# Weighting and splitting the state space inputs in small steps, and taking the mixers' elementwise work off GpSimd

## The chip, the core and the metric

The kernel runs on one core of a Trainium2 chip. A core has five engines with a queue each: TensorE (PE in the profile, with its weight loads as PEld), VectorE (DVE), ScalarE (ACT), GpSimd (POOL) and SyncE (SP, which issues DMAs). Each engine works through its own instructions in order and waits on semaphores for the others. The metric is the device time of one execution in microseconds, over several runs of the same program.

## What is computed

The reference is a model of two layers on 512 tokens of width 1024, in float32. Each layer is a mixer and a gated feed-forward network with a short convolution, both with a residual and an RMS norm ahead of them. The mixer of layer 0 joins a dilated window attention (12 heads in three groups) and a latent attention (12 heads). The mixer of layer 1 joins a state space model (16 heads in two groups, in four chunks of 128 tokens) and a stick-breaking attention (8 heads). The parts that the change touches, cut to what matters:

```python
# rotary embedding, softmax (layer 0)
x1 * cos - x2 * sin, x2 * cos + x1 * sin
p = exp(scores - m); out = (p / sum(p)) @ v
...
# state space model (layer 1), per chunk of 128 tokens
xbc = silu(causal_dwconv(xbc, conv_w, conv_b))      # 12 tiles of 128 channels
xdt = x * dt[..., None]
cs = cumsum(dt * a)
y_diag = einsum(cb[..., None] * exp(cs_l - cs_s), xdt)          # masked, causal
states = einsum(b, exp(cs_end - cs), xdt)
h = h * exp(cs_end) + states                        # over the chunks
y = y_diag + einsum(c, h_before, exp(cs)) + x * d_skip
...
# stick breaking (layer 1)
out = exp(log_w) @ v
```

## The kernel before

Activations lie with 128 channels on the partitions and the 512 tokens along the free dimension. Products run as three TensorE products of a high and a low part: every operand is split into a rounded float32r copy (ACT) and the rest (DVE or POOL), by `split` (L259), `wchunk` (L214) and `token_split` (L620). A weight chunk of 128 outputs is loaded by one DMA on SP into one of two buffers, split, and used in eight pieces of three 512 column matmuls (`proj_pieces`, L637); a piece is one step of a `Stream` (L119).

TensorE's order is written out by hand: `InOrder` (L93) chains its instructions as the program issues them. The other engines' instructions are placed by a planner, which takes dependences, buffers and its own estimate of durations into account, so a statement's place in the source sets its order there only in part. Where ACT must keep an order (its table of functions has to be loaded anew between Silu and Exp), `after` (L240) adds an edge.

A `Stream` holds the projections that still have to run. `fill(n)` (L169) takes n steps, and so places projection work between the latency bound steps of the heads. `defer(n, f)` (L155) puts f on a list, to be called n steps later; `_tick` (L159) counts all entries down, but calls only from the front of the list, so an entry that is due waits for an older one that is not.

**Layer 0's mixer** (L644). `run_qk` (L719) makes rotated queries and keys: ACT copies the projection out (L729), DVE multiplies it by the cosine in permuted order (L730), four DMAs on SP swap the halves (L733), and POOL multiplies the swapped copy by the sine (L734) and adds it (L735). There are 12 of them. The cosine and sine tiles are scaled by the norm's factor on POOL (L704). A softmax block (L572) goes: DVE masks and takes the maximum (L578), ACT takes exp with the sum (L581), DVE the reciprocal (L582), POOL scales by it (L583). There are 64 blocks, 128 to 512 wide; their probabilities are transposed on TensorE (L116), split into `pth` and `ptl` (L600, L601, L951, L952) and used.

**Layer 1's state space model** (`ssd`, L1118). The stream runs 12 convolutions (`run_conv`, L1137): tiles 0 to 7 are the inputs x, 8 and 9 the matrices B, 10 and 11 C. Each does its projection, then four steps on DVE and ACT (L1144 to L1150), Silu (L1152), and 12 steps later its transposes (`conv_tail`, L1122). `run_dt` makes the step sizes; 2 steps later `softplus` (L1184) starts, a chain of some 20 small operations on DVE; 12 steps later `summed` (L1213) takes their cumulative sums on TensorE, and 3 steps later `rows` (L1226) brings them into rows. After the last convolution (L1276) three exponentials follow (L1279), and then `prepare(0)` (L1285) for all four chunks of the first group: x times dt (`xd`, L1292, on POOL and DVE in turn), the split into `xdt` (L1296, L1297), x times d_skip (L1300, POOL), and x times dt times the decay to the chunk's end (L1302, POOL) with its split into `xe` (L1303).

Then come 16 heads (L1422). Ahead of a head stand `states` (L1307, the chunk's state, carried on with a product on POOL, L1318) and `past` (L1323, the output of earlier chunks, added on POOL, L1334), as the table `prior` (L1408) says; `weights` (L1338) makes the decay weights `sg`, `mh` of the head two places on, `apply` (L1354) multiplies them by `xdt` and adds the result to `xs`. At head 4 `prepare(1)` runs, for the second group at once. From head 8 on the gates follow (`silus`, `gate`, `gate_sums`, `gate_norm`).

**Stick breaking** (L1441). Per head and bank of blocks: `score`, with ACT and DVE on `ab` and a selection on POOL (`strict`, L1508), `sums` with another selection, the split of the weights into `wh` (L1559, DVE) and `wl` (L1560, POOL), and `apply`.

In the two feed-forward networks `self.lo` is POOL: there the low parts of the weights (L221) and one product (L528) are POOL's. In the mixers `self.lo` is DVE.

## Time and profile before

| | us |
|---|---|
| median of 3 runs | 1465.1 (1463.52 to 1468.44) |
| profiled execution | 1463.86 |
| its span, first to last instruction | 1462.1 |
| mean granted TensorE clock | 0.985 |
| stages: layer 0's mixer | 0 to 338 |
| layer 0's feed-forward network | 338 to 700 |
| convolutions of the state space model | 700 to 790 |
| its heads | 790 to 905 |
| stick breaking, with the end of the mixer | 905 to 1095 |
| layer 1's feed-forward network | 1095 to 1462 |

Times in the views are microseconds from the span's start, durations of one instruction nanoseconds; busy time is the time in which an engine has an instruction under way. A row of the stages' view has the stretch, its length, then for each engine busy time and, in brackets, its number of instructions, then the granted clock, the DMA engines' share and GB/s. A row of groups has the line, engine, operation, what is written from what, the shape, the count, the busy time, the mean duration, and the idle time of the engine before these instructions with what ended it. A row of waits names who waited for whom, the total, the number of times and the longest.

### The profile page before, as it was taken

How to read it: one execution, taken by the hardware profiler on the slowest of the kernel's cores; microseconds unless marked ns; L12 is line 12 of the kernel's file. 1: busy time of each engine (PE TensorE's matmuls, PEld its weight loads, DVE VectorE, ACT ScalarE, POOL GpSimd, SP SyncE). 2: the span in 40 equal slices, each digit the busy share in tenths (PEclk: the TensorE clock that was granted, in tenths of full speed). 3: DMA queues.
4: the chain of work that ended last, by engine and by line, in shares of the span. 5: the costliest groups of instructions: out<-in, count | busy, mean ns of one | idle time of the engine just before them, and what ended most of it. 6: DMA issues, size and time to landing. Idle time of an engine off the chain costs nothing.

```text
span 1462.1 us, 18180 instructions
## 1 busy us (share of the span) xinstructions
PE 1388.7 (95%) x6796; PEld 1146.8 (78%) x6796; DVE 863.6 (59%) x1362; ACT 663.2 (45%) x1085; POOL 597.1 (41%) x391
## 2 busy tenths in 40 slices
PE   7899899899999999999988898998999999999997
PEld 5777687687888888888877677787888888888886
DVE  7878678746555555122668987678555555552124
ACT  5557457535433333222446465777344333333222
POOL 2454445303655555444102420434215555554441
PEclk9999999999999999999999999999999999999998
DMA  4421212122322322333222111111233233223333
GB/s 166 120 62 55 69 55 69 39 81 73 101 93 95 101 101 85 105 92 95 92 72 73 44 44 58 46 58 40 62 101 101 87 102 101 91 97 94 100 98 98
DMA packets 40264, 121.22 MB, mean 83 GB/s; under 512 B 5232, under 2 KB 8304, under 8 KB 40176
## 3 DMA queue, kind: packets, MB, share of 16 engines
q1 hardware_dynamic: 38160, 117.92, 25.4%
q10 hardware_dynamic: 2016, 2.14, 0.5%
q8 instruction: 54, 0.88, 0.3%
q14 instruction: 34, 0.28, 0.1%
HBM read 114.80 MB, written 2.10 MB: 80 GB/s over the span
## 4 chain that ended last, share of the span: by engine, by line
PE 80%; DVE 12%; ACT 4%; issue 3%; POOL 1%; DMA 1%; DVEq 0%; SPq 0%; ACTq 0%; POOLq 0%
PE proj L113 50%; PE o L113 19%; PE z L113 5%; PE s L113 3%; PE t L116 2%; DVE wlo L221 2%; PE t L113 1%; ACT whi L219 1%; DVE mh L265 1%; DVE sg L1351 0%; DVE cv L1150 0%; DVE xs L1366 0%; DVE xl L331 0%; DVE s L578 0%; DVE rot L730 0%
## 5 line engine op out<-in xcount | busy, mean ns | idle before, releaser
L221 POOL TENSOR_TENSOR wlo<-wraw,whi 128x1024 fp32r<-128x1024 f32 (+1 forms) x135 | 315.2, 2336 | 323.7 <-ACT whi L219 323.7
L219 ACT ACTIVATE whi<-wraw 128x1024 fp32r<-128x1024 f32 (+3 forms) x219 | 222.2, 1015 | 365.0 <-PE proj L113 328.7
L113 PE MATMUL proj<-xh,whi 128*128 128x512 f32 x844 | 343.0, 406 | 8.8 <-ACT xh L330 6.7
L113 PE MATMUL proj<-xh,wlo 128*128 128x512 f32 x844 | 334.1, 396 | 1.4 <-DVE wlo L387 1.1
L113 PE MATMUL proj<-xl,whi 128*128 128x512 f32 x844 | 333.9, 396 | 1.2 <-DVE xl L331 1.2
L113 PE MATMUL proj<-act,whi 128*128 128x512 f32 (+1 forms) x748 | 219.3, 377 | 0.0
L113 PEld LDWEIGHTS proj<-xh,whi 128*128 128x128 f32 x844 | 161.3, 191 | 41.0 <-ACT xh L330 8.7
L113 PEld LDWEIGHTS proj<-xh,wlo 128*128 128x128 f32 x844 | 160.9, 191 | 37.6 <-DVE wlo L387 1.5
L113 PEld LDWEIGHTS proj<-xl,whi 128*128 128x128 f32 x844 | 161.2, 191 | 31.3 <-DVE xl L331 3.1
L113 PEld LDWEIGHTS proj<-act,whi 128*128 128x128 f32 x748 | 137.7, 188 | 25.8
L113 PE MATMUL o<-xh,wlo 128*128 128x512 f32 x368 | 143.4, 390 | 0.0
L113 PE MATMUL o<-xh,whi 128*128 128x512 f32 x368 | 143.3, 389 | 0.0
L113 PE MATMUL o<-xl,whi 128*128 128x512 f32 x368 | 143.2, 389 | 0.0
L113 PE MATMUL proj<-act,wlo 128*128 128x512 f32 (+1 forms) x374 | 140.8, 376 | 0.0
L583 POOL TENSOR_SCALAR s<-s,st 128x512 f32<-128x512 f32 (+1 forms) x64 | 81.2, 1274 | 109.4 <-DVE st L582 82.3
L366 DVE TENSOR_TENSOR x<-x,proj 128x512 f32<-128x512 f32 x31 | 21.2, 684 | 171.0 <-PE proj L113 170.9
L221 DVE TENSOR_TENSOR wlo<-wraw,whi 128x1024 fp32r<-128x1024 f32 (+3 forms) x84 | 100.0, 1190 | 27.3 <-ACT whi L219 26.3
L524 DVE SCALAR_TENSOR_TENSOR cv<-gt,cols,cv 128x511 f32<-128x511 f32 x44 | 94.3, 2148 | 35.9 <-ACT cv L523 35.9
L528 POOL TENSOR_TENSOR sl<-sl,rsr 128x512 f32<-128x512 f32 x44 | 57.8, 1313 | 94.3 <-ACT sl L527 94.3
L527 ACT ACTIVATE sl<-cv 128x512 f32<-128x512 f32 x44 | 27.8, 631 | 127.3 <-DVE cv L525 127.3
L533 DVE TENSOR_TENSOR up<-sl,o 128x512 f32<-128x512 f32 x44 | 30.3, 688 | 91.8 <-POOL sl L528 91.8
L265 DVE TENSOR_TENSOR act<-up,act 128x512 fp32r<-128x512 f32 x44 | 63.3, 1438 | 29.3 <-ACT act L264 29.3
(305 smaller groups left out, 2250.9 us busy)
## 6 DMA issues: line engine op xcount, KB each, us to landing
wraw<-in_g SPq DMA_DIRECT2D x44, 512.0 KB, 3.3
wraw<-in_u SPq DMA_DIRECT2D x44, 512.0 KB, 3.3
wraw<-in_d SPq DMA_DIRECT2D x32, 448.0 KB, 3.3
wraw<-in_wqk SPq DMA_DIRECT2D x20, 512.0 KB, 3.5
wraw<-in_d SPq DMA_DIRECT2D x17, 512.0 KB, 3.5
wraw<-in_wx SPq DMA_DIRECT2D x12, 512.0 KB, 3.4
wraw<-in_wv SPq DMA_DIRECT2D x10, 512.0 KB, 3.6
wraw<-in_wz SPq DMA_DIRECT2D x8, 512.0 KB, 3.3
```

What stands on the lines that cost most here:

```text
L113: return self._put(self.b.nc.tensor.matmul(*args, **kw))
L116: return self._put(self.b.nc.tensor.transpose(*args))
L219: nc.scalar.activation(hi[:, :n], raw[:, :n], AF.Copy)
L221: (eng or self.lo).tensor_tensor(lo[:, :n], raw[:, :n], hi[:, :n].bitcast(F32), op=ALU.subtract)
L265: nc.vector.tensor_tensor(lo, src, hi.bitcast(F32), op=ALU.subtract)
L366: self.nc.vector.tensor_tensor(self.x[m], self.x[m], ps, op=ALU.add)
L524: nc.vector.scalar_tensor_tensor(c[:, 1:], gt[:, : T - 1], col_(1), c[:, 1:], op0=ALU.mult, op1=ALU.add)
L527: nc.scalar.activation(s, c, AF.Silu)
L528: nc.gpsimd.tensor_tensor(s, s, r, op=ALU.mult)
L533: nc.vector.tensor_tensor(u, s, pu, op=ALU.mult)
L583: nc.gpsimd.tensor_scalar(t, t, rl, None, op0=ALU.mult)
```

## The change

It has five parts.

1. In the mixers, POOL's elementwise work goes to other engines: the scaling of the softmax to ACT (L583); the scaling of cosine and sine (L704), the product with the sine and the sum of the rotation (L734, L735), the product with the carried state (L1318), the sum of `past` (L1334) and the low part of stick breaking's weights (L1560) to DVE. POOL keeps the selections of stick breaking, some squares and mask copies at the start, and its work in the feed-forward networks.
2. `prepare` is cut into `decayed(g, c)` (x times the product of step size and decay, and its split) and `prepare(g, c, q)` (half of a chunk's heads: x times dt, its split, x times d_skip), all on DVE and ACT. `decayed` takes x times one factor, since `tok[:, 3]` is multiplied by `tok[:, 0]` beforehand.
3. For the first group both run as stream items without matmuls, after convolutions 5 and 6; for the second group they stand ahead of heads 2 to 9, by the table `early`. `past` of the second group moves to heads 10 to 12.
4. The three exponentials run as a stream item between convolutions 3 and 4, and the Silus of later convolutions are ordered behind them.
5. `_tick` calls every entry that is due, and `summed` is due after 24 steps in place of 12. The buffers of `xdt` become two sets of 4 in place of one of 8.

```diff
     def _tick(self):
         for d in self.late:
             d[0] -= 1
-        while self.late and self.late[0][0] <= 0:
-            self.late.pop(0)[1]()
+        for d in [d for d in self.late if d[0] <= 0]:
+            self.late.remove(d)
+            d[1]()
...
-        nc.gpsimd.tensor_scalar(t, t, rl, None, op0=ALU.mult)
+        nc.scalar.activation(t, t, AF.Copy, scale=rl)
...
         for t in (cr, sr):
-            nc.gpsimd.tensor_tensor(t, t, r, op=ALU.mult)
+            nc.vector.tensor_tensor(t, t, r, op=ALU.mult)
...
-                nc.gpsimd.tensor_tensor(sw, sw, sr, op=ALU.mult)
-                nc.gpsimd.tensor_tensor(view(t), view(t), view(sw, False), op=ALU.add)
+                nc.vector.tensor_tensor(sw, sw, sr, op=ALU.mult)
+                nc.vector.tensor_tensor(view(t), view(t), view(sw, False), op=ALU.add)
...
                 self.silu = nc.scalar.activation(c, c, AF.Silu)
+                for x in exps:
+                    self.after(self.silu, x)
...
-        XD = dict(tag="xdt", bufs=8)
+        XD = [dict(tag=f"xdt{q}", bufs=4) for q in range(2)]
...
+        def run_exps():
+            def run(w):
+
+                for t, src, scale in ((tok[:, 2], tok[:, 1], -1.0), (tok[:, 3], tok[:, 3], 1.0), (cdec, tot, 1.0)):
+                    exps.append(nc.scalar.activation(t, src, AF.Exp, scale=scale))
+                    self.after(exps[-1], self.silu)
+                nc.vector.tensor_tensor(tok[:, 3], tok[:, 3], tok[:, 0], op=ALU.mult)
...
+        def run_prepare(g, *cs):
+            def run(w):
+                for c in cs:
+                    if c < NB - 1:
+                        decayed(g, c)
+                    for q in range(2):
+                        prepare(g, c, q)
...
-            self.stream.defer(12, summed)
+            self.stream.defer(24, summed)
...
+        def decayed(g, c):
+
+            xd = sub.tile([P, T], F32, tag="xd", name=self.nm("xd"), bufs=2)
+            nc.vector.tensor_tensor(xd.rearrange("p (h d) -> p h d", h=8),
+                                    xs[g][:, c].rearrange("p (h d) -> p h d", h=8),
+                                    tok[:, 3, c, g * 8 : g * 8 + 8, None].to_broadcast([P, 8, 64]), op=ALU.mult)
+            xde[g, c] = self.split(xd, sub, "xe", bufs=6)
+
+        def prepare(g, c, q):
+
+            h0 = g * 8 + 4 * q
+            x4 = xs[g][:, c, q * 256 : q * 256 + 256].rearrange("p (h d) -> p h d", h=4)
+            xd = sub.tile([P, 4, 64], F32, tag=("xq", "xd")[q], name=self.nm("xq"), bufs=1 + q)
+            nc.vector.tensor_tensor(xd, x4, tok[:, 0, c, h0 : h0 + 4, None].to_broadcast([P, 4, 64]), op=ALU.mult)
+            sp = sub.tile([P, 4, 2, 64], F32R, name=self.nm("xdt"), **XD[q])
+            nc.scalar.activation(sp[:, :, 0, :], xd, AF.Copy)
+            nc.vector.tensor_tensor(sp[:, :, 1, :], xd, sp[:, :, 0, :].bitcast(F32), op=ALU.subtract)
+            xdt[g, c, q] = sp
+            nc.vector.tensor_tensor(x4, x4, dbc[:, h0 : h0 + 4, None].to_broadcast([P, 4, 64]), op=ALU.mult)
...
-                                  + [run_conv(f) for f in range(2, 8)] + others)
+                                  + [run_conv(2), run_conv(3), run_exps(), run_conv(4), run_conv(5), run_prepare(0, 0, 1),
+                                     run_conv(6), run_prepare(0, 2, 3), run_conv(7)] + others)
...
-                (nc.vector if c % 2 else nc.gpsimd).tensor_tensor(xd, x8, tq(0), op=ALU.mult)
...
-                nc.gpsimd.tensor_tensor(cur.rearrange("p (h d) -> p h d", h=8),
+                nc.vector.tensor_tensor(cur.rearrange("p (h d) -> p h d", h=8),
...
-            nc.gpsimd.tensor_tensor(xs[g][:, c], xs[g][:, c], tt, op=ALU.add)
+            nc.vector.tensor_tensor(xs[g][:, c], xs[g][:, c], tt, op=ALU.add)
...
+        for hh, f, *x in ((2, decayed, 1, 0), (3, decayed, 1, 1), (4, decayed, 1, 2),
+                          (4, prepare, 1, 0, 0), (5, prepare, 1, 1, 0), (6, prepare, 1, 2, 0), (7, prepare, 1, 3, 0),
+                          (8, prepare, 1, 0, 1), (8, prepare, 1, 1, 1), (9, prepare, 1, 2, 1), (9, prepare, 1, 3, 1)):
+            early.setdefault(hh, []).append((f, *x))
...
-                            (5, past, 0, 3), (6, states, 1, 0), (7, states, 1, 1), (8, past, 1, 1),
-                            (9, states, 1, 2), (10, past, 1, 2), (11, past, 1, 3)):
+                            (5, past, 0, 3), (6, states, 1, 0), (7, states, 1, 1), (10, past, 1, 1),
+                            (9, states, 1, 2), (11, past, 1, 2), (12, past, 1, 3)):
...
-        prepare(0)
...
-            if hh == 4:
-                prepare(1)
+            for f, *x in early.get(hh, ()):
+                f(*x)
...
-                nc.gpsimd.tensor_tensor(wl[:, :w], ab[:, :w], wh[:, :w].bitcast(F32), op=ALU.subtract)
+                nc.vector.tensor_tensor(wl[:, :w], ab[:, :w], wh[:, :w].bitcast(F32), op=ALU.subtract)
```

More of the change, by code (lines that the diff above doesn't have):

```diff
@@ L1181, in ssd @@
         nc.vector.tensor_tensor(sel, self.ident[:, 0:16], self.ident[:, 32:48], op=ALU.add)
-        ready = []
+        ready, exps = [], []
+        def run_exps():
[4 more added lines that the diff above has]
+                nc.vector.tensor_tensor(tok[:, 3], tok[:, 3], tok[:, 0], op=ALU.mult)
+                return
+                yield
+            return "exps", lambda: None, run
+        def run_prepare(g, *cs):
[5 more added lines that the diff above has]
+                        prepare(g, c, q)
+                return
+                yield
+            return f"p{g}{cs[0]}", lambda: None, run
         def softplus():
@@ L1263, in run_cb @@
             return f"cb{g}", lambda: None, run
+        xdt, xde = {}, {}
+        def decayed(g, c):
[14 more added lines that the diff above has]
+            nc.vector.tensor_tensor(x4, x4, dbc[:, h0 : h0 + 4, None].to_broadcast([P, 4, 64]), op=ALU.mult)
         st = self.stream = Stream([run_conv(8), run_conv(10), run_conv(9, "o"), run_dt(), run_conv(11, "o"),
                                    run_conv(0)] + [run_cb(0), run_conv(1), run_cb(1)]
-                                  + [run_conv(f) for f in range(2, 8)] + others)
+                                  + [run_conv(2), run_conv(3), run_exps(), run_conv(4), run_conv(5), run_prepare(0, 0, 1),
+                                     run_conv(6), run_prepare(0, 2, 3), run_conv(7)] + others)
         cm = sub.tile([P, P], BF16, tag="cm", name="cm")
@@ L1277, in ssd @@
         assert ready
-        for t, src, scale in ((tok[:, 2], tok[:, 1], -1.0), (tok[:, 3], tok[:, 3], 1.0), (cdec, tot, 1.0)):
-            self.after(nc.scalar.activation(t, src, AF.Exp, scale=scale), self.silu)
         st.fill(4)
-        xdt, xde = {}, {}
-        def prepare(g):
-            xds = []
-            for c in range(NB):
-                x8 = xs[g][:, c].rearrange("p (h d) -> p h d", h=8)
-                tq = lambda k: tok[:, k, c, g * 8 : g * 8 + 8, None].to_broadcast([P, 8, 64])
-                xd = sub.tile([P, 8, 64], F32, tag="xd", name=self.nm("xd"), bufs=2)
-                (nc.vector if c % 2 else nc.gpsimd).tensor_tensor(xd, x8, tq(0), op=ALU.mult)
-                for q in range(2):
-                    h4 = slice(4 * q, 4 * q + 4)
-                    sp = sub.tile([P, 4, 2, 64], F32R, name=self.nm("xdt"), **XD)
-                    nc.scalar.activation(sp[:, :, 0, :], xd[:, h4], AF.Copy)
-                    nc.vector.tensor_tensor(sp[:, :, 1, :], xd[:, h4], sp[:, :, 0, :].bitcast(F32), op=ALU.subtract)
-                    xdt[g, c, q] = sp
-                nc.gpsimd.tensor_tensor(x8, x8, dbc[:, g * 8 : g * 8 + 8, None].to_broadcast([P, 8, 64]), op=ALU.mult)
-                if c < NB - 1:
-                    nc.gpsimd.tensor_tensor(xd, xd, tq(3), op=ALU.mult)
-                    xde[g, c] = self.split(xd.rearrange("p h d -> p (h d)"), sub, "xe", bufs=6)
         state = {}
@@ L1405, in gate_norm @@
                                                op0=ALU.mult, op1=ALU.mult)
-        prior, later = {}, {}
+        prior, later, early = {}, {}, {}
+        for hh, f, *x in ((2, decayed, 1, 0), (3, decayed, 1, 1), (4, decayed, 1, 2),
+                          (4, prepare, 1, 0, 0), (5, prepare, 1, 1, 0), (6, prepare, 1, 2, 0), (7, prepare, 1, 3, 0),
+                          (8, prepare, 1, 0, 1), (8, prepare, 1, 1, 1), (9, prepare, 1, 2, 1), (9, prepare, 1, 3, 1)):
+            early.setdefault(hh, []).append((f, *x))
         for hh, f, g, c in ((0, states, 0, 0), (1, states, 0, 1), (2, past, 0, 1), (3, states, 0, 2), (4, past, 0, 2),
-                            (5, past, 0, 3), (6, states, 1, 0), (7, states, 1, 1), (8, past, 1, 1),
-                            (9, states, 1, 2), (10, past, 1, 2), (11, past, 1, 3)):
+                            (5, past, 0, 3), (6, states, 1, 0), (7, states, 1, 1), (10, past, 1, 1),
+                            (9, states, 1, 2), (11, past, 1, 2), (12, past, 1, 3)):
             prior.setdefault(hh, []).append((f, g, c))
-        prior[8].append((silus, 0))
+        prior.setdefault(8, []).append((silus, 0))
         prior[14] = [(silus, 1)]
```

6 lines of the change are left out of this document (3 added, 3 removed).

## The prediction

> **What bounds the kernel now.** I read the busy shares and the chain that ended last, then PE's waits, then the stages the change touches.
>
> ```profile
> PE 1388.7 (95%) x6796; PEld 1146.8 (78%) x6796; DVE 863.6 (59%) x1362; ACT 663.2 (45%) x1085; POOL 597.1 (41%) x391
> ...
> PE 80%; DVE 12%; ACT 4%; issue 3%; POOL 1%; DMA 1%; DVEq 0%; SPq 0%; ACTq 0%; POOLq 0%
> ```
>
> PE's order is written out by hand, PE is busy 1388.7 of 1462.1 us, and the chain is PE's wherever PE is not waiting for DVE (12%). So an edit gains only what it takes out of PE's idle time. The stages (columns: length, then busy us of PE, PEld, DVE, ACT, POOL, then the granted clock):
>
> ```profile
> 60.00:338.00 278.00, 253.49 (x1523) 207.96 (x1522) 202.99 (x480) 157.60 (x323) 115.16 (x86) 0.99 0.21 63
> ...
> 700.00:750.00 50.00, 46.14 (x224) 37.82 (x223) 35.61 (x71) 25.33 (x42) 3.40 (x3) 0.93 0.23 77
> 750.00:790.00 40.00, 40.00 (x194) 33.26 (x194) 29.71 (x38) 20.81 (x31) 3.94 (x3) 1.00 0.26 83
> 790.00:830.00 40.00, 32.31 (x151) 25.29 (x150) 35.28 (x47) 23.05 (x55) 18.32 (x15) 0.91 0.14 50
> 830.00:870.00 40.00, 36.41 (x180) 28.58 (x179) 36.02 (x57) 24.05 (x52) 13.39 (x10) 0.96 0.12 40
> 870.00:905.00 35.00, 31.72 (x185) 26.64 (x185) 29.49 (x61) 20.84 (x41) 1.66 (x1) 1.00 0.18 60
> 905.00:1045.00 140.00, 130.18 (x647) 108.37 (x647) 102.26 (x170) 93.46 (x162) 54.56 (x73) 0.98 0.15 48
> ```
>
> 60 to 338 is the even mixer, 700 to 790 the convolutions, 790 to 905 the state space heads, 905 to 1045 stick breaking. From 700 to 905 PE idles 3.86 + 0 + 7.69 + 3.59 + 3.28 = 18.4 us. The clock falls too: (1 - 0.93) x 50 = 3.5, 0.09 x 40 = 3.6, 0.04 x 40 = 1.6, together 8.7 us. So 27 us are lost here, 7.4 in the first stage and 19.8 from 790 on; PE's own work is 205 - 27 = 178 us. What ends the long waits (total, times, longest):
>
> ```profile
> PE s L113 <- DVE sp L1211: 3.9, 1, 3.9
> ...
> PE o L113 <- DVE xdt L1297: 6.4, 2, 3.9
> ...
> PE o L113 <- DVE ptl L601: 5.1, 4, 1.8
> ...
> PE t L116 <- POOL s L583: 2.1, 3, 1.1
> ```
>
> The first is the softplus chain, not done when `summed` comes up; the second is `prepare(0)`, in one burst ahead of the first `apply`. In that burst:
>
> ```profile
> 797.32 0.68 DVE L1351 TENSOR_TENSOR sg<-sg,cb 128x512 f32<-128x512 f32 x1
> 797.92 1.53 DVE L265 TENSOR_TENSOR mh<-sg,mh 128x512 fp32r<-128x512 f32 x1
> ...
> 800.82 0.68 DVE L1315 COPY stt<-t 128x512 f32<-128x512 f32 x1
> 801.42 0.67 DVE L265 TENSOR_TENSOR mh<-sg,mh 128x512 fp32r<-128x512 f32 x1
> 802.02 1.52 DVE L1292 TENSOR_TENSOR xd<-xs,tok 128x512 f32<-128x512 f32 x1
> ```
>
> Back to back, a 512 wide DVE operation takes 0.60 us from start to start (801.42 to 802.02). The same `mh` takes 1.53 us in one place and 0.67 in another: DVE stands still while POOL holds something both need.
>
> **The softplus chain.** `summed` goes from 12 to 24 pieces, and the new `_tick` lets `softplus` (due after 2 pieces) run without waiting for older entries of the list. One piece is three matmuls, by the chain of waits:
>
> ```profile
> 384.38 5.44 PE proj L113 x24
> ```
>
> 5.44 / 24 = 0.227 us each, 0.68 a piece. DVE is 3.9 us late; 12 more pieces are some 8 us, and `softplus` itself starts earlier, since its entry no longer stands behind the transposes of a convolution that are due after 12 pieces. What is late next would be the three exponentials and `rows`; they stand two convolutions later. Gain 7 of the 7.4 us (bounds 4 to 7.4).
>
> **The state space inputs.** Groups from 700 to 905 (xcount | busy, mean ns | idle):
>
> ```profile
> L265 DVE TENSOR_TENSOR mh<-sg,mh 128x512 fp32r<-128x512 f32 x16 | 13.3, 834 | 0.9 <-ACT mh L264 0.9
> L1366 DVE TENSOR_TENSOR xs<-o,xs 128x256 f32<-128x256 f32 x32 | 13.3, 417 | 2.1 <-POOL xs L1334 1.2 <-PE o L113 0.5
> L1297 DVE TENSOR_TENSOR xdt<-xd,xdt 128x256 fp32r<-128x256 f32 x16 | 10.7, 711 | 0.5 <-ACT xdt L1296 0.5
> L265 DVE TENSOR_TENSOR ph<-stt,ph 128x512 fp32r<-128x512 f32 x6 | 6.5, 1081 | 0.7 <-ACT ph L264 0.7
> L265 DVE TENSOR_TENSOR xe<-xd,xe 128x512 fp32r<-128x512 f32 x6 | 5.6, 952 | 0.0
> L1292 DVE TENSOR_TENSOR xd<-xs,tok 128x512 f32<-128x512 f32 x4 | 5.3, 1319 | 0.0
> ...
> L1334 POOL TENSOR_TENSOR xs<-xs,yof 128x512 f32<-128x512 f32 x6 | 10.0, 1669 | 23.4 <-DVE yof L1332 23.4
> L1300 POOL TENSOR_TENSOR xs<-xs,hb 128x512 f32<-128x512 f32 x8 | 9.6, 1202 | 2.9 <-DVE xd L1292 2.6
> L1302 POOL TENSOR_TENSOR xd<-xd,tok 128x512 f32<-128x512 f32 x6 | 6.8, 1144 | 24.4 <-ACT tok L1280 16.7 <-DVE xdt L1297 7.7
> L1318 POOL TENSOR_TENSOR stt<-stt,cdec 128x512 f32<-128x512 f32 x4 | 5.6, 1404 | 8.5 <-DVE stt L1320 5.7 <-DVE stt L1315 2.8
> ```
>
> DVE gains 6 + 6 + 4 = 16 operations of 0.60 us (L1334, L1302, L1318): 9.6. A 256 wide one is 417 ns less the same 0.08 of overlap, 0.34 us: L1300 becomes 16 of them (5.4), and L1292 becomes 16 in place of DVE's 4 of 512 (5.4 - 2.4 = 3.0). Together +18.0 us. Against that stand the waits for POOL, mean over clean: `mh` 16 x 0.15, `xdt` 16 x 0.29, `ph` 6 x 0.40, `xe` 6 x 0.27, `xd` 4 x 0.64 = 13.6 us. (The clean values are 0.68 for 512 and 0.42 for 256, from the rows above.) DVE so goes from 166.1 to 170 us beside 178 us of PE work: the load hardly grows, but it has no room. The ACT copies stay 16 and no DMA is added. The places fit the buffers: `prepare(1, c, 0)` at heads 4 to 7 takes the buffers that heads 0 to 3 have read, `prepare(1, c, 1)` at heads 8 and 9 those of heads 4 to 7, and each is needed one to four heads later, a head being some 7 us (115 / 16); so no wait comes in there unless DVE itself runs a head behind. In DVE's queue these 0.34 us pieces stand ahead of `sg` and `mh` of the next weights, for which PE waits, but never more than some 2 us of them at a time, where the burst held 2 `xd`, 8 `xdt` and 3 `xe`, 2 x 1.32 + 8 x 0.71 + 3 x 0.95 = 11. About 11.6 us of it (`prepare(0)` and its three `decayed`) now fall between convolution 5 and the heads, where DVE has a quarter free; PE may pay 1 us. The nearest row for what remains is 870 to 905, POOL nearly silent and DVE 84% busy: PE idles 3.28 of 35, 9%. Over some 105 us of heads that leaves 10 of the 19.8 us. Gain 10 - 1 = 9 (bounds 0, with DVE as the bound, to 19.8). The exponentials placed between convolutions cost two more table loads:
>
> ```profile
> L581 ACT ACT_TABLE_LOAD  x1: 1283/1283/1283, 69.4 to 69.4; - x1
> ```
>
> 2.6 us on ACT, 20.81 of 40 busy there; behind them waits one Silu, whose transposes come 12 pieces later: nothing. Without that cover, 2.6.
>
> **The even mixer.** Durations (min/median/max, and from issue to landing):
>
> ```profile
> L733 SPq DMA_DIRECT2D sw<-raw x48: 507/584/1465, 43.3 to 228.9; - x48
> L734 POOL TENSOR_TENSOR sw<-sw,sin x12: 1282/1292/1692, 47.3 to 233.8; 128x512 f32<-128x512 f32 x12
> L735 POOL TENSOR_TENSOR rot<-rot,sw x12: 1372/1559/1919, 48.7 to 236.7; 128x512 f32<-128x512 f32 x12
> ...
> POOL sw L734: 20.8, 5
> ...
> DMA to landing us min/median/max: 1.9/2.0/3.9
> L583 POOL TENSOR_SCALAR s<-s,st 128x512 f32<-128x512 f32 (+1 forms) x64 | 81.2, 1274 | 109.4 <-DVE st L582 82.3
> L264 ACT ACTIVATE qk<-rt 128x512 fp32r<-128x512 f32 x12 | 7.6, 630 | 3.9 <-DVE rt L773 3.9
> L730 DVE TENSOR_TENSOR rot<-proj,cos 128x512 f32<-128x512 f32 x12 | 11.9, 994 | 0.1
> L872 DVE TENSOR_TENSOR kl<-knp,kh 64x512 fp32r<-64x512 f32 x12 | 10.6, 880 | 0.8 <-ACT kh L871 0.6
> ```
>
> The 64 scalings go to ACT, at most 64 x 0.63 = 40 us on 157.60 of 278, and each softmax is ready 0.6 us sooner. In ACT's queue each now waits for DVE's reciprocal, with Exp, `pth` and `whi` behind it. DVE takes 14 plain products (two of L704) at 0.60 and 12 permuted sums, as L730 does, at 0.9: 19 us, less waits for POOL of perhaps 0.2 x 12 (`kl`) and as much again elsewhere: net +14 on 202.99 of 278. And it takes over a wait: four copies in a row on SP, 3 x 0.58, then 2.0 to land, come to 4 us, for which POOL sat idle 20.8 us before 5 of the 12; the other 7 it covered with scalings. In DVE's queue `ptl`, `vt` and `wlo` stand behind it. If the order puts it far enough back, it is free; right behind L730 it costs some 3 us x 12 = 36. I take 0.75 each, 9 us of DVE, and a third of it on PE: +3. Bounds: -9 (the `ptl` and `s` waits gone, 5.1 + 2.1, and some clock) to +24 (two thirds of 36).
>
> **Stick breaking.** 24 subtractions (L1560) go from POOL to DVE at most at 0.60: +14 us on 102.26 of 140, less some waits; POOL's selections, which stay, no longer stand behind them. The 384 wide ones, two thirds of the 24:
>
> ```profile
> L1560 POOL TENSOR_TENSOR wl<-ab,wh 128x384 fp32r<-128x384 f32 x16 | 18.6, 1162 | 11.3 <-DVE wh L1559 9.9 <-PE proj L113 1.4
> ```
>
> Each product of weights and values is so ready some 0.6 us sooner, and DVE carries 14 us more; PE idles 9.8 of 140 us here, and I let the two nearly cancel: -1 (bounds -5, half of that idle time, to +8, the added DVE work as far as no wait for POOL goes away and half of it shows).
>
> **Sum.** -7 - 9 + 3 - 1 = -14 us on the profiled execution's 1463.9, which is 1.2 below the median of 1465.1: 1451 on the median's scale.
>
> **Rivals.**
> (a) All of it works: DVE's queue is freer than its sum says and the softmaxes gain: -7 - 15 - 7 - 2 = -31, 1434. For it: 13.6 us of waits for POOL vanish just where PE waits. Against: DVE at 170 of 178.
> (b) DVE becomes the bound of the heads: only the first 7 us and 1 us of stick breaking come, the mixer takes 3: 1460. For it: DVE is 88 and 90% busy from 790 to 870.
> The Trainium skill, Perfetto Trace Analysis, Optimizing Scalar/DVE Operations, speaks for (b): where DVE is saturated, work should go off it, even to GpSimd, though the two share a port, so that moving between them may not help. By that rule the time would be that of (b). The trace bears it out in half: DVE is nearly full, but 1.53 against 0.67 us shows that a move off POOL gives waits back.
> (c) Slower: the rotations' products stand in DVE's queue ahead of their copies. Price 2 us of PE each, 24 us, in place of 3: 1472. It decides from 17 us on, 1.4 us a rotation. For it: the 20.8 us of POOL; against: DVE has other work to be placed ahead.
> (d) No change: stalls are only handed to the next stage, 1465.
>
> **Chances.** Forecast 0.42, (a) 0.22, (b) 0.12, (c) 0.13, (d) 0.11. A difference under 0.3%, 4.4 us, can't be told from none here. Faster 0.42 + 0.22 + 0.12 less 0.02 for (b)'s upper edge = 0.74, within 0.13, slower 0.13. The range reaches to (a) and halfway to (c): 1433 to 1467.
>
> **What would show it.** Right: no wait of PE for `sp`, full clock from 700 to 905, that stage near 189 us, DVE about 90% busy in it, `mh` and `ph` near 0.68 us. Wrong: DVE idle ahead of L734 with a DMA as its releaser; DVE at 97% among the heads; ACT idle ahead of L583; PE waiting for `xdt` again.

## The result, and the profile after

| | before | after |
|---|---|---|
| median, us (4 runs each) | 1465.28 (1463.52 to 1468.44) | 1454.86 (1453.63 to 1456.0) |
| profiled execution, us | 1463.86 | 1454.47 |
| its span, us | 1462.1 | 1452.7 |
| mean granted clock | 0.985 | 0.991 |

The ratio is 0.9919, with a 95% interval of 0.9899 to 0.9939: 10.4 us faster, where 14 were forecast. The page of the changed kernel, in the same two lines as before (busy time by engine; the chain that ended last):

```profile
PE 1384.7 (95%) x6796; PEld 1142.2 (79%) x6796; DVE 880.2 (61%) x1457; ACT 697.2 (48%) x1151; POOL 413.2 (28%) x249
...
PE 79%; DVE 12%; ACT 5%; issue 2%; DMA 1%; POOL 0%; SPq 0%; DVEq 0%; ACTq 0%; POOLq 0%
```

POOL lost 184 us of work (597.1 to 413.2); DVE gained 17, ACT 34. The chain hardly looks different, so the stages have to tell. Here both kernels are cut where PE's own program passes from one part to the next, so that a row holds the same matmuls in each (the counts agree but for a few lost records). The six rows are layer 0's mixer, its feed-forward network, the convolutions, the heads, stick breaking, the rest; the columns are those of the stages' view above. Before:

```profile
0.00:337.10 337.10, 302.39 (x1748) 246.89 (x1749) 249.94 (x563) 188.41 (x369) 134.43 (x107) 0.99 0.26 79
337.10:717.50 380.40, 379.50 (x1690) 314.26 (x1689) 172.64 (x178) 130.78 (x166) 188.13 (x93) 1.00 0.30 95
717.50:789.20 71.70, 67.84 (x324) 55.57 (x323) 51.76 (x82) 38.11 (x59) 3.94 (x3) 0.95 0.23 76
789.20:908.30 119.10, 103.76 (x527) 82.93 (x524) 103.12 (x170) 69.55 (x148) 33.38 (x25) 0.96 0.15 49
908.30:1042.40 134.10, 125.07 (x625) 104.48 (x626) 99.47 (x161) 91.23 (x160) 54.56 (x73) 0.97 0.15 47
1042.40:1462.10 419.70, 410.12 (x1891) 342.69 (x1889) 186.68 (x212) 145.12 (x185) 182.69 (x91) 0.99 0.31 97
```

After:

```profile
0.00:343.60 343.60, 304.79 (x1749) 246.83 (x1750) 261.55 (x589) 220.06 (x433) 16.37 (x17) 0.99 0.26 78
343.60:722.40 378.80, 377.86 (x1690) 312.97 (x1689) 172.80 (x178) 130.91 (x166) 188.12 (x93) 1.00 0.30 95
722.40:793.30 70.90, 67.00 (x324) 54.38 (x323) 57.64 (x108) 43.80 (x71) 0.00 (x0) 0.98 0.23 77
793.30:905.10 111.80, 103.03 (x526) 84.05 (x523) 96.25 (x189) 66.23 (x138) 0.00 (x0) 0.95 0.16 52
905.10:1033.50 128.40, 122.41 (x624) 101.65 (x625) 104.63 (x184) 91.19 (x160) 26.05 (x49) 1.00 0.16 49
1033.50:1452.70 419.20, 409.65 (x1891) 342.31 (x1889) 187.37 (x213) 145.00 (x185) 182.69 (x91) 0.99 0.30 97
```

A row gives two things. Its length less PE's busy time is PE's **idle time**. And because the matmuls are the same, a difference in PE's busy time is read here as time lost to a **lower clock**. After less before:

| stage | length | idle | busy (clock) |
|---|---|---|---|
| layer 0's mixer | +6.5 | 34.7 to 38.8: +4.1 | +2.4 |
| feed-forward network | -1.6 | 0 | -1.6 |
| convolutions | -0.8 | 3.9 to 3.9: 0 | -0.8 |
| heads | -7.3 | 15.3 to 8.8: -6.6 | -0.7 |
| stick breaking | -5.7 | 9.0 to 6.0: -3.0 | -2.7 |
| rest | -0.5 | 0 | -0.5 |
| sum | -9.4 | -5.5 | -3.9 |

So the two stages of the state space model give 8.1 us, not 16; stick breaking gives 5.7, not 1; and the mixer takes 6.5, not 3. The 1.6 us of layer 0's feed-forward network, where the change touches nothing, are read as chance of the clock: that stage takes 380.4 us in two of the fourteen profiles of this document (before and b_stick) and 378.7 to 378.8 in the others.

What ends PE's waits after (total, times, longest). Convolutions:

```profile
PE t L116 <- ACT cv L1153: 3.9, 2, 2.4
```

Heads:

```profile
PE o L113 <- DVE mh L266: 6.1, 4, 3.0
```

Layer 0's mixer, before (the wait for `s` on POOL is in the prediction) and after:

```profile
PE proj L113 <- DVE vt L759: 4.5, 4, 1.4
PE t L116 <- DVE ptl L952: 2.9, 1, 2.9
PE s L113 <- DVE qk L265: 2.4, 1, 2.4
PE t L116 <- DVE v L629: 1.4, 3, 0.7
```

```profile
PE proj L113 <- DVE vt L760: 5.6, 5, 1.6
PE s L113 <- DVE qk L266: 3.8, 2, 2.8
PE t L116 <- DVE ptl L953: 3.8, 1, 3.8
PE t L116 <- ACT s L584: 3.7, 5, 1.4
PE t L116 <- DVE v L630: 2.9, 4, 0.9
```

The waits for `sp` and for `xdt` are gone, as forecast. In the convolutions a Silu (L1153) has taken the place of `sp`, for the very same 3.9 us; in the heads `mh` is what is late. In the mixer PE waits a little longer for each of five things, 6.5 us more in all; two other waits became shorter (`ptl` of L601, now L602, 5.1 to 2.6, and `rot`, 3.6 to 1.8).

The new wait in the convolutions can be read instruction by instruction. ACT's timeline of the changed kernel (start, length, what it does, in brackets the idle time ahead of it and its releaser):

```profile
766.78 1.28 ACT L1191 ACT_TABLE_LOAD   x1
...
775.77 1.28 ACT L1153 ACT_TABLE_LOAD   x1 [1.42 <-DVE cv L1151]
777.06 0.63 ACT L1153 ACTIVATE cv<-cv 128x512 f32<-128x512 f32 x1
```

And PE's, just behind it:

```profile
777.74 1.11 PE L116 MATMUL t<-ident,cv 128*128 128x128 f32 x4 [2.39 <-ACT cv L1153]
...
779.51 0.63 PE L113 MATMUL proj<-xh,wlo 128*128 128x512 f32 x1
779.94 0.63 PE L113 MATMUL proj<-xh,whi 128*128 128x512 f32 x1
...
781.32 0.39 PE L113 MATMUL proj<-xl,whi 128*128 128x512 f32 x1
781.55 0.39 PE L113 MATMUL proj<-xh,wlo 128*128 128x512 f32 x1
```

The table, which ACT had changed for the exponentials (L1191), is loaded back for Silu only when DVE has finished the convolution's last tap, and DVE carries 5.9 us more in this stage (51.76 to 57.64). So the load's 1.28 us stand on the path, and PE waits 2.39. Behind that wait the matmuls come 0.43 us apart (779.51 to 779.94), where they come 0.23 apart later (781.32 to 781.55): the stall costs a stretch at half clock as well.

### The profile page after: what moved, and what is told of

It reads as the page before. It is cut to its first block, busy times and chain, and to the rows that moved or that the text cites. A ratio compares the mean times of both kernels' runs of the same rounds, so it can differ in the third digit from the quotient of the medians.

```text
span 1452.7 us, 17971 instructions
## 1 busy us (share of the span) xinstructions
PE 1384.7 (95%) x6796; PEld 1142.2 (79%) x6796; DVE 880.2 (61%) x1457; ACT 697.2 (48%) x1151; POOL 413.2 (28%) x249
## 4 chain that ended last, share of the span: by engine, by line
PE 79%; DVE 12%; ACT 5%; issue 2%; DMA 1%; POOL 0%; SPq 0%; DVEq 0%; ACTq 0%; POOLq 0%
PE proj L113 49%; PE o L113 19%; PE z L113 5%; PE s L113 2%; DVE wlo L222 2%; PE t L116 2%; PE t L113 1%; ACT whi L220 1%; DVE cv L1151 1%; ACT s L584 1%; DVE xl L332 0%; ACT s L582 0%; DVE x L367 0%; DMA sw<-raw 0%; DVE ab L1559 0%
## 5 line engine op out<-in xcount | busy, mean ns | idle before, releaser
L113 PEld LDWEIGHTS proj<-xh,wlo 128*128 128x128 f32 x844 | 160.2, 190 | 37.5 <-DVE wlo L388 1.5
L222 DVE TENSOR_TENSOR wlo<-wraw,whi 128x1024 fp32r<-128x1024 f32 (+3 forms) x84 | 95.6, 1138 | 28.7 <-ACT whi L220 27.9
L113 PEld LDWEIGHTS proj<-act,wlo 128*128 128x128 f32 x374 | 70.4, 188 | 12.9
```

Source lines behind the costliest of these rows:

```text
L113: return self._put(self.b.nc.tensor.matmul(*args, **kw))
L222: (eng or self.lo).tensor_tensor(lo[:, :n], raw[:, :n], hi[:, :n].bitcast(F32), op=ALU.subtract)
```

## The experiments

Two theories of the state space burst are put against each other. **Work on POOL**: the state space burst was slow because POOL held DVE up, and taking work off POOL made the heads faster (that spreading the burst does it was put to a_burst). **Place of the exponentials**: the burst was slow because it could not begin until the exponentials behind the last Silu had run, and what the change gained there it gained by moving those. Twelve kernels were run; each ratio is to the kernel before, measured beside it. The kernel before had medians of 1465.2, 1465.6, 1466.4 and 1468.0 us in the four sets, so medians of different sets are best compared by their ratios.

| kernel | median, us | ratio (95%) |
|---|---|---|
| b_softplus | 1458.17 | 0.9946 (0.9927 to 0.9965) |
| b_stick | 1459.46 | 0.9961 (0.9947 to 0.9975) |
| b_even | 1473.05 | 1.0049 (1.0034 to 1.0065) |
| b_two | 1452.12 | 0.9892 (0.9876 to 0.9909) |
| b_exps | 1463.95 | 0.9992 (0.9978 to 1.0006) |
| a_burst | 1455.78 | 0.9930 (0.9903 to 0.9958) |
| a_ssd_pool | 1452.82 | 0.9916 (0.9891 to 0.9940) |
| a_edge | 1455.38 | 0.9932 (0.9912 to 0.9951) |
| a_tail16 | 1455.29 | 0.9931 (0.9908 to 0.9955) |
| a_even_pool | 1448.47 | 0.9884 (0.9866 to 0.9902) |
| a_rot_pool | 1449.79 | 0.9886 (0.9862 to 0.9911) |
| best | 1449.52 | 0.9887 (0.9865 to 0.9908) |

Names with b_ are the kernel before with one part of the change, names with a_ the changed kernel with one part undone or altered. PE's idle time by stage, worked out from each one's stage rows as above:

| kernel | mixer | convolutions | heads | stick breaking |
|---|---|---|---|---|
| before | 34.7 | 3.9 | 15.3 | 9.0 |
| after | 38.8 | 3.9 | 8.8 | 6.0 |
| b_softplus | 34.7 | 0.0 | 15.3 | 9.8 |
| b_stick | 34.5 | 3.9 | 15.3 | 5.9 |
| b_even | 36.8 | 3.9 | 15.7 | 9.8 |
| b_two | 33.1 | 0.0 | 15.3 | 6.0 |
| b_exps | 33.8 | 7.5 | 9.7 | 9.8 |
| a_burst | 37.3 | 3.9 | 8.8 | 5.9 |
| a_ssd_pool | 37.7 | 2.2 | 9.0 | 5.9 |
| a_edge | 37.0 | 3.0 | 10.7 | 6.0 |
| a_tail16 | 37.5 | 0.0 | 13.8 | 6.0 |
| a_even_pool | 32.7 | 3.9 | 10.1 | 6.0 |
| a_rot_pool | 34.4 | 3.9 | 8.4 | 6.0 |
| best | 34.4 | 0.0 | 12.1 | 6.0 |

### The softplus chain alone (b_softplus)

```diff
-        while self.late and self.late[0][0] <= 0:
-            self.late.pop(0)[1]()
+        for d in [d for d in self.late if d[0] <= 0]:
+            self.late.remove(d)
+            d[1]()
...
-            self.stream.defer(12, summed)
+            self.stream.defer(24, summed)
```

> The kernel before with only the new list handling and the sums due after 24 pieces. Stage reading of the two traces: in the changed kernel the wait of PE for the softplus chain (3.9 us and half a clock for 6.8 us) is gone, but other waits came up in the convolutions. If the stall is its own loss: 7 us faster than before (about 1458 us). If it is only handed on to the burst ahead of the heads, which is DVE's: within 2 us of before, with the wait for xdt grown by as much.

Measured: 1458.17 against 1465.22, so 7.1 us. The stage rows of the convolutions and the heads:

```profile
716.50:781.60 65.10, 65.10 (x323) 53.31 (x322) 50.68 (x82) 37.92 (x59) 3.95 (x3) 1.00 0.24 84
781.60:900.90 119.30, 104.03 (x527) 83.12 (x525) 102.91 (x170) 69.51 (x148) 34.36 (x25) 0.96 0.15 49
```

PE is never idle in the convolutions (65.10 of 65.10) and has the full clock; the stage is 6.6 us shorter than before, and the heads are as they were (119.3 against 119.1). This term was right, and nothing is late next. The two parts of the edit were not run apart. The chain's last product starts 24.4 us into the stage in place of 26.5, so by these times its earlier start covers some 2.1 of the 3.9 us, and the later `summed` the rest.

### Stick breaking alone (b_stick)

```diff
-                nc.gpsimd.tensor_tensor(wl[:, :w], ab[:, :w], wh[:, :w].bitcast(F32), op=ALU.subtract)
+                nc.vector.tensor_tensor(wl[:, :w], ab[:, :w], wh[:, :w].bitcast(F32), op=ALU.subtract)
```

> The kernel before with only the low part of stick breaking's weights on DVE. In the changed kernel this stage became 5.7 us shorter where 1 was forecast. If the move itself does it (POOL's selections no longer stand behind the subtractions): 4 to 6 us faster than before, 1460. If the stage was shorter because of what came ahead of it (waits and clock): within 1.5 us of before.

Measured: 5.8 us, from one line. The stage row, and the wait of ACT that moved, of this kernel:

```profile
908.30:1036.70 128.40, 122.50 (x625) 101.65 (x626) 104.57 (x184) 91.20 (x160) 26.26 (x49) 1.00 0.15 49
```

```profile
ACT ab L1528 <- DVE wl L1560: 6.2, 5, 2.6
```

The same wait, and PE's two waits for the scores' parts, in the kernel before:

```profile
ACT ab L1528 <- POOL wl L1560: 9.7, 8, 2.6
```

```profile
PE z L113 <- DVE sl L1536: 4.4, 3, 1.6
...
PE z L113 <- DVE sh L1535: 1.4, 2, 0.7
```

DVE's work in the stage went from 99.47 to 104.57 us, 5.1 and not the 14 that were counted for the moved line: the line did bring 14.3 us, but other operations became shorter (the 384 wide `sh` 502 to 364 ns, `sl` 624 to 566, `q` 804 to 684). ACT's next bank waits 9.7 - 6.2 = 3.5 us less for the buffer that the subtraction reads, PE's idle time falls by 3.1, and its busy time by 2.6: the clock is full (1.00, 0.97 before). The split depends on the profile that it is taken against: in b_softplus, b_even and b_exps, with the old line, the stage has 9.8 us of idle time and 123.7 of busy time, and against these 3.9 us are idle time and 1.2 clock.

### Layer 0's mixer alone (b_even), and the change without it (a_even_pool)

```diff
-        nc.gpsimd.tensor_scalar(t, t, rl, None, op0=ALU.mult)
+        nc.scalar.activation(t, t, AF.Copy, scale=rl)
...
-            nc.gpsimd.tensor_tensor(t, t, r, op=ALU.mult)
+            nc.vector.tensor_tensor(t, t, r, op=ALU.mult)
...
-                nc.gpsimd.tensor_tensor(sw, sw, sr, op=ALU.mult)
-                nc.gpsimd.tensor_tensor(view(t), view(t), view(sw, False), op=ALU.add)
+                nc.vector.tensor_tensor(sw, sw, sr, op=ALU.mult)
+                nc.vector.tensor_tensor(view(t), view(t), view(sw, False), op=ALU.add)
```

That is b_even; a_even_pool is the changed kernel with these lines as they were.

> The kernel before with only layer 0's mixer changed: softmax scaling on ACT, rotation and norm factor on DVE. If the mixer's 6 us of loss come from these moves: 5 to 7 us slower than before, about 1471. If they are chance of this stage's clock and waits: within 2 us of before.

> The changed kernel with layer 0's mixer as before: softmax scaling, rotation and norm factor on GpSimd again. The same three moves alone cost 7.8 us on the kernel before. If that loss adds to the rest: 7 to 8 us faster than the changed kernel, 1447. If the later stages take it back, since they start from another state of clock and loads: within 2 us of the changed kernel.

Measured: alone the part costs 7.8 us (1473.05 against 1465.22), and without it the changed kernel is 6.4 us faster (1448.47 against 1454.86; by the two ratios, 0.9884 and 0.9919, 5.1). Both have the same sign, and both are more than the +3 of the prediction. Not all of it lies in the mixer: in b_even's profile the mixer is 9.2 us longer than before, and the heads of layer 1, which the edit doesn't touch, 3.2 (122.3 for 119.1), nearly all of that in busy time. The stage row of a_even_pool:

```profile
0.00:335.80 335.80, 303.07 (x1748) 246.55 (x1749) 248.94 (x563) 188.33 (x369) 134.16 (x107) 0.99 0.27 80
```

PE idles 32.7 us in it, 38.8 in the changed kernel.

### Only the rotation back on GpSimd (a_rot_pool)

```diff
-                nc.vector.tensor_tensor(sw, sw, sr, op=ALU.mult)
-                nc.vector.tensor_tensor(view(t), view(t), view(sw, False), op=ALU.add)
+                nc.gpsimd.tensor_tensor(sw, sw, sr, op=ALU.mult)
+                nc.gpsimd.tensor_tensor(view(t), view(t), view(sw, False), op=ALU.add)
```

> The changed kernel with only the rotation's product and sum on GpSimd again; the softmax scaling stays on ACT. All of layer 0's moves together cost 6.4 to 7.8 us. If the rotation on DVE costs it (DVE's load, and its waits for the copies): 5 to 7 us faster than the changed kernel, 1449. If the scaling on ACT costs it (each waits in ACT's queue for DVE's reciprocal, with other work behind it): within 2 us of the changed kernel, 1455.

Measured: 0.9886, next to 0.9884 for the whole mixer undone. The mixer's row:

```profile
0.00:343.60 343.60, 309.23 (x1749) 250.54 (x1750) 250.76 (x565) 219.88 (x433) 52.17 (x41) 0.98 0.25 78
```

By its length this row says that nothing was gained (343.6, as after). Read in two parts it says something else: idle 34.4, which lies in the 32.7 to 34.7 of the seven profiles whose mixer is the old one, and not in the 36.8 to 38.8 of the six whose mixer is the new one; and 4.4 us more busy time for the same matmuls (309.23 against 304.79), which is read as clock. ACT's 219.88 us show that the softmax scaling is still there. So the idle time belongs to the rotation, and the scaling on ACT costs none that can be told from nothing. Why the clock was lower in this profile isn't known: in profiles with the new mixer the busy time ranges from 304.79 (after) to 309.48 (b_even), with the old one from 302.39 (before) to 308.10 (best).

The gain in total proves less. This profile is 3.2 us shorter than the changed kernel's, and the heads alone are 3.4 shorter (108.4 for 111.8), with PE's busy time at 100.00 for 103.03. The planner had put DVE's instructions there in another order, in some twenty places, though the edit is in the mixer.

What the rotation costs DVE, in the changed kernel's mixer:

```profile
L736 DVE TENSOR_TENSOR rot<-rot,sw 128x512 f32<-128x512 f32 x12 | 12.2, 1018 | 0.1
L735 DVE TENSOR_TENSOR sw<-sw,sin 128x512 f32<-128x512 f32 x12 | 8.3, 688 | 2.7 <-DMA sw<-raw 2.5
```

The wait for the copies is 2.5 us in all, not 9. What remains is the work itself, 12.2 + 8.3 = 20.5 us in the one queue that `vt`, `qk`, `ptl` and `v` also go through; four of the five waits that grew are for these. That the work makes them late is argued, not shown: the planner also ordered DVE's other work in the mixer anew, and no run tells the two apart.

### The exponentials between the convolutions, nothing else (b_exps)

```diff
+                for x in exps:
+                    self.after(self.silu, x)
...
-                                  + [run_conv(f) for f in range(2, 8)] + others)
+                                  + [run_conv(2), run_conv(3), run_exps()] + [run_conv(f) for f in range(4, 8)] + others)
...
-        for t, src, scale in ((tok[:, 2], tok[:, 1], -1.0), (tok[:, 3], tok[:, 3], 1.0), (cdec, tot, 1.0)):
-            self.after(nc.scalar.activation(t, src, AF.Exp, scale=scale), self.silu)
```

> The kernel before with only the three exponentials moved between convolutions 3 and 4; the preparation stays as it was, on GpSimd and DVE. With the last chunks' xd in two buffers that are held until a product with an exponential has read them, the third chunk can't start before the exponentials. If this makes the burst: the wait of PE for xdt (6.4 us) goes, the heads become 7 us shorter, 1458. If GpSimd's hold on DVE makes it: the wait stays and the time is within 2 us of before.

Measured: 0.9992, no change. But the stage rows of the convolutions and heads are not those of before:

```profile
720.10:800.80 80.70, 73.23 (x323) 58.96 (x322) 59.30 (x89) 44.35 (x71) 12.97 (x9) 0.89 0.21 68
800.80:911.20 110.40, 100.69 (x526) 81.55 (x524) 96.11 (x163) 65.91 (x138) 26.96 (x19) 0.98 0.16 53
```

```profile
PE s L113 <- DVE sp L1223: 3.9, 1, 3.9
PE t L116 <- ACT cv L1152: 3.6, 2, 3.4
```

The heads take 110.4 us instead of 119.1, with `prepare` still in its two forms of before, half of it on POOL: idle 15.3 to 9.7, of the 15.3 to 8.8 that the whole change brings. PE no longer waits for `xdt`. So the mechanism of the first expectation came, with the time of the second. The planner moves the burst ahead by itself once the exponentials are out of the way. One explanation, argued from the code: each of the two buffers of `xd` is held until its product with an exponential (L1302) is done, so the third chunk could not start before them. The convolutions take 80.7 instead of 71.7: DVE carries 7.5 us more there (59.30 for 51.76), and PE waits for Silu (3.6) beside `sp` (3.9), with a clock of 0.89. The gain was handed back one stage earlier.

### The preparation in bursts again (a_burst)

```diff
-                                     run_conv(4), run_conv(5), run_prepare(0, 0, 1),
-                                     run_conv(6), run_prepare(0, 2, 3), run_conv(7)] + others)
+                                     run_conv(4), run_conv(5),
+                                     run_conv(6), run_conv(7)] + others)
...
+        for c in range(NB):
+            if c < NB - 1:
+                decayed(0, c)
+            for q in range(2):
+                prepare(0, c, q)
...
+        for hh, f, *x in ([(4, decayed, 1, c) for c in range(3)] + [(4, prepare, 1, c, 0) for c in range(4)]
+                          + [(8, prepare, 1, c, 1) for c in range(4)]):
```

> The changed kernel with the first group's inputs prepared in one burst after the convolutions again, the second group's in two bursts at heads 4 and 8; all of it stays on DVE and ACT. If spreading is what gains in the heads: 8 to 15 us slower than the changed kernel, 1463 to 1470, with waits of PE for xdt of 6 us or more back. If taking the work off POOL gains it (DVE no longer stands still for POOL): within 3 us of the changed kernel, since the waits that came up in the convolutions go away in exchange.

Measured: 0.9930 (0.9903 to 0.9958), and the order of the instructions on DVE, ACT and POOL is the same as in the changed kernel (but for one record that is missing). So spreading the calls in the source does nothing; the planner sets where they run. What one burst would cost after the exponentials have moved isn't shown, since this run has none. The two are one program measured twice, which shows how far two measurements of it differ: 0.9919 and 0.9930, idle 38.8 and 37.3 in the mixer, 8.8 and 8.8 in the heads.

### Four products of the heads back on GpSimd (a_ssd_pool)

```diff
-            nc.vector.tensor_tensor(xd.rearrange("p (h d) -> p h d", h=8),
+            nc.gpsimd.tensor_tensor(xd.rearrange("p (h d) -> p h d", h=8),
...
-            nc.vector.tensor_tensor(x4, x4, dbc[:, h0 : h0 + 4, None].to_broadcast([P, 4, 64]), op=ALU.mult)
+            nc.gpsimd.tensor_tensor(x4, x4, dbc[:, h0 : h0 + 4, None].to_broadcast([P, 4, 64]), op=ALU.mult)
...
-                nc.vector.tensor_tensor(cur.rearrange("p (h d) -> p h d", h=8),
+                nc.gpsimd.tensor_tensor(cur.rearrange("p (h d) -> p h d", h=8),
...
-            nc.vector.tensor_tensor(xs[g][:, c], xs[g][:, c], tt, op=ALU.add)
+            nc.gpsimd.tensor_tensor(xs[g][:, c], xs[g][:, c], tt, op=ALU.add)
```

> The changed kernel with four of the state space products on GpSimd again: x times decay, x times d_skip, the carried state, the sum of the earlier chunks; order of the steps and exponentials stay as changed. If taking work off GpSimd gains in the heads: 4 to 10 us slower than the changed kernel, 1459 to 1465, with DVE's mh and ph again at 0.8 us and more. If the place of the exponentials gained it: within 2 us of the changed kernel, or faster, since DVE has less to do.

Measured: 0.9916, no slower than the changed kernel's 0.9919. The groups of DVE in the convolutions and heads (count, busy, mean), first in the changed kernel, then in this one:

```profile
L1376 DVE TENSOR_TENSOR sg<-sg,cb 128x512 f32<-128x512 f32 x16 | 10.9, 684 | 2.7 <-ACT sg L1373 2.6
L266 DVE TENSOR_TENSOR mh<-sg,mh 128x512 fp32r<-128x512 f32 x16 | 10.9, 682 | 0.1
```

```profile
L1376 DVE TENSOR_TENSOR sg<-sg,cb 128x512 f32<-128x512 f32 x16 | 13.2, 826 | 2.8 <-ACT sg L1373 2.8
L266 DVE TENSOR_TENSOR mh<-sg,mh 128x512 fp32r<-128x512 f32 x16 | 11.5, 720 | 0.8 <-ACT mh L265 0.7
```

With POOL at work DVE's operations are slower again (before the change they took 799 and 834); with POOL silent DVE has more of them. Its busy time in the heads is 96.25 one way and 96.90 the other, and PE's idle time in both stages together 12.7 and 11.1. The work-on-POOL theory falls here. The Trainium skill (Perfetto Trace Analysis, Optimizing Scalar/DVE Operations) says that the two share a port, so that moving operations between them might not help; for these four products the runs agree.

### Two tries to keep both gains (a_edge, a_tail16)

a_edge holds the second halves of the first group's preparation back behind the taps of the last convolution:

```diff
-                    for q in range(2):
-                        prepare(g, c, q)
+                    prepare(g, c, 0)
...
+        for c in range(NB):
+            prepare(0, c, 1, self.taps)
...
+            if late is not None:
+                self.after(i, late)
```

> The changed kernel with the second halves of the first group's inputs (heads 4 to 7) held back by an order edge on DVE until the last convolution's taps are done. In the changed kernel PE waits 3.9 us for the Silu of two convolutions, where DVE works on those halves. If they delay the convolutions: these waits and half a clock for 3.4 us go, 4 to 5 us faster than the changed kernel, 1450. If DVE is as full in the heads: the wait moves there, within 1.5 us of the changed kernel.

a_tail16 lets the transposes of convolutions 3 to 7 come 16 steps after the convolution, not 12:

```diff
-                    self.stream.defer(F_N[2], lambda: conv_tail(f, c))
+                    self.stream.defer(16 if 3 <= f < 8 else F_N[2], lambda: conv_tail(f, c))
```

> The changed kernel with the transposes of convolutions 3 to 7 due 16 pieces after them in place of 12, some 2.7 us of PE work later. PE there waits 3.9 us for Silu, which stands behind the exponentials, a table load and DVE's fuller queue. If that wait is PE's loss: 3 to 5 us faster than the changed kernel, 1451. If the inputs come too late for the heads by as much: within 1.5 us.

Measured: 0.9932 and 0.9931, neither told from the changed kernel. The stage rows of a_tail16, and what PE waits for in its heads:

```profile
723.20:787.90 64.70, 64.70 (x320) 52.83 (x319) 52.18 (x97) 42.15 (x69) 0.00 (x0) 1.00 0.24 84
787.90:905.50 117.60, 103.85 (x530) 84.56 (x529) 101.73 (x200) 67.62 (x141) 0.00 (x0) 0.96 0.14 50
```

```profile
PE o L113 <- DVE mh L266: 4.8, 6, 1.5
PE o L113 <- ACT mh L265: 3.7, 2, 3.3
```

The convolutions lose their stall (70.9 to 64.7) and the heads gain one (111.8 to 117.6). Part of the stall has only changed rows: the last four transposes now fall behind the boundary (320 matmuls ahead of it for 324), and PE still waits 1.8 us for a Silu there. The rest is mostly a longer wait for ACT's part of `mh` (0.6 to 3.7). One reading is that PE's projection steps can cover DVE's work only once: what the convolutions use of them, the heads lack. Together the two stages stay at 182.3 to 182.7 us.

### Sums of parts (b_two, best)

b_two is the kernel before with the edits of b_softplus and of b_stick and nothing else. best is a_even_pool with the edits of a_ssd_pool and a_tail16.

> The kernel before with the two parts that gained by themselves: the sums due after 24 pieces with the new list handling (7.1 us), and the low part of stick breaking's weights on DVE (5.8 us). Added up: 1452.5. The changed kernel with layer 0's mixer as before differs from this one only in the state space inputs, their exponentials and products; it took 1448.5. If these edits gain 4 us of their own: 1452 to 1453. If they only hand PE's loss from the heads to the convolutions, as the stages say (190.8 us before, 182.8 after, 184.4 with the sums alone): 1448 to 1450.

> The changed kernel with layer 0's mixer as before, four state space products on GpSimd again, and the transposes of convolutions 3 to 7 due after 16 pieces. If the effects of the single runs add up (6.4, 2 and 4 us): 1443. If they overlap: 1447, no faster than layer 0's mixer alone.

Measured: 0.9892 (0.9876 to 0.9909) and 0.9887 (0.9865 to 0.9908). So two small edits, without anything done to the state space inputs, give at least all that the changed kernel gives (0.9919); and what the restructured inputs add to them is the step from b_two to a_even_pool, 0.9892 to 0.9884, which the intervals don't tell from nothing (nor, by themselves, from 4 us). By PE's idle time in the convolutions and heads it is 15.3 to 14.0, 1.3 us. b_two's forecast can't be read from its median: 1452.12 would speak for a gain of the inputs' own, but the kernel before took 1468.0 in this set, and by the ratio the time is 1449.5 on the scale of 1465.3, which speaks for stalls handed on. best reached neither 1443 nor 1447; the effects don't add up. The fastest medians are those of a_even_pool, best and a_rot_pool, 1448.5 to 1449.8, and b_two's ratio can't be told from theirs.

## Why the prediction was right, and where it was wrong

The total was right (-10.4 for -14, well within the range), and so was the sign; of its four terms one was right, one failed in its mechanism, and two had the wrong size. That the total came so near is partly luck: against the sum, the profiles show the state space stages 7.9 us and the mixer 3.5 us worse, stick breaking 4.7 us better, and 2.1 us gained in stages that the change doesn't touch. The premise that "an edit gains only what it takes out of PE's idle time" was too narrow: 3.9 of the 9.4 us are busy time.

- **Softplus, -7: right.** Alone it gives 7.1 us, with PE's 3.9 us of waiting and the slow clock behind it gone. "What is late next" was where it slipped: nothing is late in b_softplus, but in the full change the same stage gets a wait of 3.9 us for a Silu, so that there the term can't be seen (idle 3.9 before and after).
- **The state space inputs, -9: the step failed.** The prediction laid the burst's length on waits for POOL and on its being in one piece. The place in the source turned out to have no effect (a_burst), and four of POOL's products none (a_ssd_pool). What moved the burst was the step that was costed at nothing, the exponentials: in b_exps they alone bring the heads from 15.3 to 9.7 us of idle time, near the 10 us that the prediction let remain, and cost 3.6 in the convolutions. Why they hold the burst (the two buffers of `xd`) is argued only. The two table loads were said to be hidden by 12 steps of cover, "without that cover, 2.6"; the cover was used up while DVE did the burst's work at the same time, and one load of 1.28 us stood on the path. Beside the softplus term the inputs are worth some 1 us.
- **Heads at 9% idle: near.** 8.8 of 111.8 is 8%. The waits of DVE for POOL did vanish (`mh` 834 to 682 ns), and DVE's work in both stages stayed the same (154.9 to 153.9 us, forecast +4). DVE was busy 153.9 / 182.7 = 84% of them, not 90. That arithmetic was good; what it left out was that the wait would move to the convolutions: the two stages went from 190.8 to 182.7 us, where 16 less would have been 174.8.
- **Layer 0's mixer, +3: mis-sized.** +7.8 alone, +6.4 in the full change. The wait for the copies, taken as 9 us of DVE, was 2.5, so rival (c), which priced that wait at 24 us, had a wrong mechanism though the right sign for this part. The work was counted nearly right (+14; DVE's busy time rose by 11.6; L736's 1018 ns, less the 0.08 us of overlap that the prediction takes off, are 0.94 us for the 0.9 assumed). Too small was the share that reaches PE: idle time grew by 4.1 us in the profile. Another 2.4 us are busy time, which the term didn't hold at all; profiles of one and the same mixer differ in it by 5 us, so how much of that the move causes stays open.
- **Stick breaking, -1: mis-sized.** -5.8. The 14 us for DVE were 5.1 net, because waits for POOL went away, and "I let the two nearly cancel" had no ground. The lower bound, -5, was half of PE's idle time and again left out the clock: 3.1 us of idle time and 2.6 of clock were gained against the profile before, 3.9 and 1.2 against three others with the old line.
- **Rivals.** (a), all of it works, would have needed the mixer to gain; (b), DVE as the bound of the heads, gave 1460 and missed stick breaking; its rule about moving work off POOL holds for four products. (d), stalls handed on, was right for the convolutions and heads taken by themselves (b_exps, a_tail16) and wrong for the whole. The range's upper end, 1467, isn't "halfway to (c)": half of the way from 1451 to 1472 is 1461.5.

Open: why PE's busy time in the mixer differs from one profile to another by up to 5 us at the same order of work; and which of DVE's products behind the rotation costs PE how much.

## What to carry to other kernels

Cut both profiles where the bounding engine passes the same instruction and split each stage into its idle and its busy time: the first is the schedule, the second the clock, and a stage that looks unchanged can hold a gain and a loss. Where a planner orders the work, ask what an instruction depends on and which buffer it needs, not where it stands in the source. Before adding a preparation to a stage, count the cover that its own consumers already use there: here a stall cured in the heads came back in the convolutions, and two small edits gave as much as the whole change. Where a planner orders the work, check too whether an edit has changed the order in stages that it doesn't touch.

## What the runs showed of the hardware

A stall can cost more than its length. In the changed kernel, after the 2.39 us without a matmul that end at 777.74, matmuls came 0.43 us apart until about 780.8 (granted clock 0.50) and 0.23 apart after that (1.00). The Trainium skill (TensorE: Matmul & The Clock Gate, Part 1: The HAM clock gate) describes a half rate after an idle window of about 3.4 us that runs free of the kernel. The half rate and the length of the slow stretch agree with it; a gap of 2.39 us was enough here, shorter than that window, and a second gap of 1.52 us in the same stage brought none (the matmuls behind it came 0.23 apart):

```profile
786.85 0.66 PE L116 MATMUL t<-ident,cv 128*128 128x128 f32 x4 [1.52 <-ACT cv L1153]
```

These gaps give no threshold, though. In layer 0's feed-forward network one and the same wait of 0.24 us is in the kernel before and in b_softplus:

```profile
349.82 0.50 PE L113 MATMUL proj<-xh,wlo 128*128 128x512 f32 x1 [0.24 <-POOL wlo L221]
```

```profile
350.50 0.51 PE L113 MATMUL proj<-xh,wlo 128*128 128x512 f32 x1 [0.24 <-POOL wlo L222]
```

Behind it the kernel before has a granted clock of 0.50 from 351 to 353 and matmuls 0.43 us apart, b_softplus 1.00 and 0.23. So a part of what differs between two profiles isn't explained by the waits, and a difference of two or three microseconds in one profile's busy time needs a second profile.

A sum whose operands are read in permuted order takes DVE longer than one in plain order: of the twelve of L736, all of 128 x 512, the ten permuted ones took 1.07 to 1.11 us in the changed kernel, the two plain ones 0.68 and 0.69, as the plain products of L735 did (688 ns).
